# One RWKV mixer: the key projection cut in two, and the chunks' preparation written in another order around the scan

## The chip, the cores and the metric

The program runs on one core of a Trainium2 chip. The metric is the device time of one execution in microseconds (us), lower being better. The core has a matrix engine (TensorE, PE in the profile), a vector engine (VectorE, DVE), a scalar engine (ScalarE, ACT), GpSimd (POOL) and the queues that issue transfers (SP above all, and ACT). Each of them works through its own list of instructions in the order in which they stand, and waits where an input or a buffer is not there yet.

## The reference

Two layers on 256 context and 256 latent tokens of width 1024: attention with a mixture of experts, then an RWKV-7 mixer with a mixture of experts. The change lies in the mixer alone:

```python
r = heads(mix(0) @ w_r)
k = heads(mix(2) @ w_k)
v = heads(mix(3) @ w_v)
kk = k * heads(k_k)
kk = kk * lax.rsqrt(jnp.maximum(jnp.sum(kk * kk, axis=-1, keepdims=True), 1e-24))
for d in range(2):
    ...
    ins = (r, decay, k_d, v, -kk, kk * iclr)
    s_ctx, y_c = wkv_scan(zero, *(t[:, :L] for t in ins), reverse=reverse)
    _, y_l = wkv_scan(s_ctx, *(t[:, L:] for t in ins), reverse=reverse)

def step(s, inp):
    r_t, w_t, k_t, v_t, a_t, b_t = inp
    sa = jnp.einsum('bhvk,bhk->bhv', s, a_t)
    s = s * w_t[:, :, None, :] + sa[..., None] * b_t[:, :, None, :] + v_t[..., None] * k_t[:, :, None, :]
    return s, jnp.einsum('bhvk,bhk->bhv', s, r_t)
```

There are 16 heads of 64 and two directions `d`; the recurrence runs over the context tokens, then over the latent ones.

## The kernel before

The mixer is a list of steps in `rwkv` (L1236), each a function. The list is the order in which the program is written down. A scheduler then sets the order on each engine: it takes an instruction when its inputs are there by its own reckoning, the earlier-written one first, and it gives buffers of a pool out in written order. So where a step stands in the list also decides which buffer it has to wait for.

- `l` (`loras`): decay and learning-rate projections, stored to DRAM as `sgs` and `ics`. Their pool `loras` is closed at `h`; the pools `solve` and `hats` take its memory.
- `K` (`proj_k`): the key projection in four column groups n = 0 to 3. Each is a string of matmuls (L148 to L150, three for one product in full precision) and a closing part, `k_sink`: squares, head sums (L1410), a power on POOL, transposes (L1419), a spread of the factor over 64 rows (L1424), a product (L1425), and stores to `kks`. The closing part works in two PSUM banks, tag `k`.
- `R`, `gate`, `V`: the other projections. `R` evicts into tiles of the tags `kr` and `k1`, four buffers each, which `k_sink` uses too (L1404, L1440), `gate` also (L1542). All accumulators have the four PSUM banks of tag `L`; `V` needs all four at once.
- `H0` to `H3` (`wkv_hat`): for a chunk u of 128 tokens of each direction, four hat groups (direction d by half kh of the heads). A group loads `kk`, `sig`, `icl`, takes the decay sums on PE (L1585, in tag `k` while the projections run), exponentials on ACT, products on DVE and POOL, stores `hA` and `hB`, and closes with 16 matmul rows (L1624, G below) that ACT evicts into the chunk's matrix `AB[u]`. In H0 and H1 all groups share one set of buffers (`Ep`, `Em`, `A`, `BK`, `icl` one each), so they follow one another.
- `S0` to `S3` (`wkv_solve`): the inverse of a chunk's triangular matrices: 65 DVE rows in a chain (one transpose, 62 small products and sums at L1658 and L1660, two transposes), then four short runs on PE (L1682, L1686) with ACT between.
- `c0` to `c7` (`wkv_scan`): the eight scan steps of 64 tokens, each needing the state `Z` of the one before (last rows L1835 or L1838) and the solve of its chunk: S0 for c0 and c1, S1 for c2 and c3, S2 for c4 and c5, S3 for c6 and c7. `M4` to `M7` prepare the last four.
- `close`: the projections' pools end; the solves' PSUM bank and the scan's pools open.

Of the kernel before, what the change touches and what calls it, by code (L numbers as in the profile page):

```python
# [28 lines left out]
def shape_constants():  # L29
    c = {}  # L30
    t = np.arange(256)
    pos = np.stack([t // 64, t % 64], -1).astype(np.float32)
    inv = (np.float32(10000.0) ** (-np.arange(16, dtype=np.float32) / np.float32(16))).astype(np.float32)
    ang = (pos[:, :, None] * inv).astype(np.float32)
    cos, sin = np.cos(ang).astype(np.float32), np.sin(ang).astype(np.float32)
    c["cos"] = np.stack([cos, cos], 2).reshape(2, 128, 64).transpose(1, 0, 2).reshape(128, 128)
    c["sin"] = np.stack([-sin, sin], 2).reshape(2, 128, 64).transpose(1, 0, 2).reshape(128, 128)
    i, j = np.arange(128)[:, None], np.arange(128)[None, :]
    c["band"] = np.concatenate([np.where(j <= i, 0, NEG), np.where(j >= i, 0, NEG)], 1)
    c["ident"] = np.eye(128)  # L40
    c["before"] = i < j
    c["iota"] = np.broadcast_to(np.arange(384), (128, 384))
    e = np.arange(16)
    c["erev"] = np.broadcast_to(16 - e, (128, 16))
    c["grev"] = np.broadcast_to(4 - np.arange(4), (128, 4))
    lt = np.arange(128) % 64
    lc = np.arange(128) // 64
    tri = np.zeros((2, 128, 2, 65))
    for q in range(2):
        inq = (lc == q)[:, None]  # L50
        t = np.arange(64)[None, :]
        m0 = (lt <= 31)[:, None] * inq
        m1 = (lt >= 32)[:, None] * inq
        tri[0, :, q, 0:1] = -1.0 * m0
        tri[0, :, q, 1:65] = (lt[:, None] <= t) * inq - 1.0 * m0
        tri[1, :, q, 0:64] = (lt[:, None] >= t) * inq - 1.0 * m1
        tri[1, :, q, 64:65] = -1.0 * m1
    c["tri0"], c["tri1"] = tri[0].reshape(128, 130), tri[1].reshape(128, 130)
    t = np.arange(64)[None, :]
    c["gm0"], c["gm1"] = lt[:, None] <= t, lt[:, None] >= t  # L60
    c["gmk"] = np.where(np.arange(128)[:, None] < 64, lt[:, None] > t, lt[:, None] < t)
    c["e4"] = (i == np.arange(256)[None, :] // 64)
    c["hsel"] = (i // 64 == np.arange(2)[None, :])
    late = ("tri0", "tri1", "gm0", "gm1", "gmk", "hsel", "e4")
# [15 lines left out]
class Net:  # L80
# [1107 lines left out]
    def rwkv(self, st, se, sf):  # L1188
# [44 lines left out]
        lo = self.pool(slo, "loras", side="right")  # L1233
        self.Z, self.main, self.y2, self.late, wk = [None, None], {}, [], [], None
        self.trit = "k"
        for o in ["l", "K", "h", "H0", "R", "H1", "Vm", "gate", "V", "hx", "close", "S0", "H2", "S1", "c0", "H3", "x", "S2", "c1", "S3", "c2", "c3", "M4", "n", "c4", "M5", "c5", "M6", "c6", "M7", "c7", "F"]:  # L1236
            u = int(o[1]) if len(o) == 2 and o[1].isdigit() else None
            if o == "h":
                slo.close()
                vp.append(self.pool(ssv, "solve", side="right"))  # L1240
                hp["w"] = self.pool(shat, "hats", side="right")
                self.abd(hp["w"])
                self.hp = [hp["w"]]
            elif o == "hx":
                shx.close()
                hp["x"] = self.pool(shat, "hatsX", side="right")
                self.abd(hp["x"])
                self.hp = [hp["x"], hp["w"]]
            elif o == "close":
                sproj.close()  # L1250
                self.open_psum(smain, s=1)
                self.open_psum(shat, "right", t=1)
                self.trit = "t"
                vp.append(self.pool(smain, "solveX"))
                wk = self.bk = self.pool(smain, "wkv")
                self.open_psum(smain, **{t: BUFS[t] for t in "ac" if BUFS[t]})
                self.hat_tiles("A", wk)
            elif o == "l":
                self.loras(lo, h)
            elif o == "K":  # L1260
                self.proj_k(h)
            elif o == "R":
                self.proj_r(h)
            elif o == "V":
                if not V:
                    V.append(self.mix_split(3, h))
                self.proj_v(*V[0])
            elif o == "Vm":
                V.append(self.mix_split(3, h))
            elif o == "gate":  # L1270
                self.gate_hidden(h)
            elif o[0] == "H":
                q = int("0011"[u])
                self.AB.append(vp[q].tile([128, 2, 16, 64], F32, tag="AB", bufs=2 if q == 0 else 2, name=self.uid("AB")))
                self.wkv_hat(u, self.AB[-1])
            elif o[0] == "S":
                self.wkv_solve(vp[int("0101"[u])], u, self.AB[u])
            elif o == "x":
                shat.close()
                self.open_psum(smain, "right", m=2)  # L1280
                self.alias = {k: v.split() for k, v in {"y": "a"}.items()}
                self.wl = self.pool(smain, "wkvL")
                self.hat_tiles("R", self.wl)
                y2 = self.wl.tile([128, 2, D], F32, name="y2")
                self.y2 = [y2[:, t, :] for t in range(2)]
            elif o == "n":
                ssv.close()
                nring = self.pool(st, "ringN", bufs=1, side="right")
                yy = nring.tile([128, 2, D], F32, tag="yf", bufs=3, name="yy")
                y += [yy[:, t, :] for t in range(2)]  # L1290
                self.rings((nring, 1))
            elif o[0] == "M":
                self.main[u] = self.wkv_mains(wk, u)
            elif o[0] == "c":
                self.wkv_scan(wk, u, y)
            elif o == "F":
                tail = self.out_factors(nring)
# [87 lines left out]
                    ws = slice(b * width, (b + 1) * width)  # L1385
                    yield m * c + a + b, wh[:, ws], wl[:, ws]

    def proj_k(self, h):
        mh, ml = self.mix_split(2, h)
        for n in range(4):  # L1390
            acc = [self.ps(tag="L") for _ in range(2)]
            for k, wh, wl in self.wsplit("rwkv_w_k", n, 256):
                for q in range(2):
                    qs = slice(q * 128, q * 128 + 128)
                    self.mm3(acc[q], wh[:, qs], wl[:, qs], mh[k], ml[k], k == 0, k == KT - 1)
            self.k_sink(n, acc)

    def k_sink(self, n, acc):
        nc = self.nc
        pn = self.ps((128, 4, 2, 2), tag="k")  # L1400
        out = []
# [15 lines left out]
        pt = self.ps((4, 512), tag="k")  # L1417
        for t in range(4):
            nc.tensor.transpose(pt[:, t * 128:(t + 1) * 128], rn[:, t, :], self.ident)  # L1419
        rT = self.lp.tile([4, 512], F32, tag="rT", bufs=2, name=self.uid("rT"))  # L1420
        nc.vector.tensor_copy(rT, pt)
        for i, ts in enumerate(out):
            pb = self.ps(tag="k")
            nc.tensor.matmul(pb, self.cst("e4")[0:4, i * 128:i * 128 + 128], rT, start=True, stop=True)  # L1424
            nc.vector.tensor_tensor(out=ts[0], in0=ts[0], in1=pb, op=ALU.mult)  # L1425
            for a, t in enumerate(ts):
                nc.scalar.dma_start(out=self.kks[:, a, 2 * n + i], in_=t.rearrange("p (v t) -> p v t", v=2))
# [123 lines left out]
    Bs = {0: slice(0, 64), 1: slice(64, 128)}  # L1551
    Ks = {0: slice(64, 128), 1: slice(0, 64)}

    def wkv_hat(self, u, AB):
        nc = self.nc
        CD = float(np.exp(np.float32(-0.5)))
        lat = u >= 2
        for d in range(2):
# [6 lines left out]
            mid, end = (0, 64) if d == 0 else (64, 0)  # L1565
            v4 = lambda t: t.rearrange("p k (c t) -> p k c t", c=2)
            fm = self.fm[d, u]
            for kh in range(2):
                wk = self.hp[(2 * d + kh) % len(self.hp)]
                ks = slice(4 * kh, 4 * kh + 4)  # L1570
                kk = self.ht(wk, "kk", [128, 2, 4, 128])
# [45 lines left out]
                nc.vector.tensor_tensor(out=kd, in0=kd, in1=icl, op=ALU.mult)  # L1617
                nc.gpsimd.tensor_tensor(out=bk(Ks), in0=v4(kd), in1=Em[:, :, :, inc], op=ALU.mult)
                nc.sync.dma_start(out=self.hB[d, u][:, :, ks, :], in_=BK)
                for lc in range(2):  # L1620
                    p = self.ps((128, 4, 128), tag="G")
                    q64 = slice(64 * d, 64 * d + 64)
                    for q in range(4):
                        nc.tensor.matmul(p[q64, q, :], BK[:, lc, q, Bs] if d == 0 else A[:, lc, q, :],  # L1624
                                         Abd[:, lc, q].rearrange("p a t -> p (a t)"),
                                         start=True, stop=True, skip_group_check=True)
                    pq = p.rearrange("p q (a t) -> p (q a) t", a=2)
                    for jb in range(2):
# [490 lines left out]
```

## Time and profile before

| | before |
|---|---|
| median of 3 runs | 1976.08 us (1969.65 to 1979.23) |
| the profiled execution | 1968.82 us |
| its span, first to last instruction | 1967.0 us |
| PE busy over the span | 1703.4 us, 87% |
| DVE, ACT, POOL busy | 972.1, 729.0, 321.9 us |
| mean granted TensorE clock | 0.936 |

The span is what the trace shows, some 2 us less than the execution's time. The mixer runs from about 908 to 1440 us; ahead of it and behind it the two mixtures of experts stream weights.

### The profile page before, as it was taken

What the parts mean: (1) busy time and instruction counts of PE and PEld (TensorE: products, weight loads), DVE (VectorE), ACT (ScalarE), POOL (GpSimd) and SP (SyncE); (2) the same over time, 40 slices, a digit from 0 to 9 for tenths busy, and PEclk for the clock granted to TensorE, in tenths of its full rate; (3) what the DMA queues carried; (4) which work ended last, traced back from release to release, by engine and by line L of the source; (5) the groups of instructions that cost most, each with busy time, mean ns of one, the idle gap of its engine ahead of it and who ended that gap; (6) DMA issues with size and microseconds to landing.
All of it is one profiled execution on the core that took longest, in us unless ns stands there. A gap on an engine that the chain in (4) does not pass through costs nothing. (4 is left out here: it accounts for less than half of the span.)

```text
span 1967.0 us, 30330 instructions
## 1 busy us (share of the span) xinstructions
PE 1703.4 (87%) x11673; PEld 1037.8 (53%) x11673; DVE 972.1 (49%) x1864; ACT 729.0 (37%) x1379; POOL 321.9 (16%) x313
## 2 busy tenths in 40 slices
PE   5978997889999999994898978889777999988986
PEld 3845565645555555552577767879653333322321
DVE  2466555756555555657745589973653111110101
ACT  2324543545444554543545765642141000100000
POOL 2040032000000000014557353510330000000000
PEclk7989998899999999997898987889988999999999
DMA  8377766699999999995357878635395999999996
GB/s 335 108 295 255 264 186 236 224 356 410 409 410 410 407 409 365 378 361 150 108 186 226 274 209 239 197 102 125 120 392 225 409 409 409 410 408 409 409 409 274
DMA packets 232019, 585.95 MB, mean 298 GB/s; under 512 B 43131, under 2 KB 87443, under 8 KB 231862
## 3 DMA queue, kind: packets, MB, share of 16 engines
q1 hardware_dynamic: 213446, 545.46, 75.2%
q10 hardware_dynamic: 15536, 27.92, 3.9%
q0 software_dynamic: 2880, 10.49, 1.5%
q8 instruction: 96, 1.57, 0.3%
q14 instruction: 61, 0.50, 0.1%
HBM read 544.19 MB, written 39.63 MB: 297 GB/s over the span
## 5 line engine op out<-in xcount | busy, mean ns | idle before, releaser
L143 DVE TENSOR_TENSOR lo<-raw,hi 128x512 fp32r<-128x512 f32 x456 | 305.2, 713 | 208.3 <-ACT hi L142 203.1
L142 ACT ACTIVATE hi<-raw 128x512 fp32r<-128x512 f32 x488 | 292.3, 628 | 215.2 <-PE ps L150 148.1
L1122 PE MATMUL ps<-raw,XT 128*64 128x512 f32 x1024 | 233.5, 597 | 15.3 <-DMA raw<-in_moe_w_dram 15.3
L1122 PEld LDWEIGHTS ps<-raw,XT 128*64 128x64 f32 x1024 | 72.2, 136 | 170.2 <-issue 125.6
L1128 DVE TENSOR_TENSOR h<-h,ps 128x512 f32<-128x512 f32 x16 | 11.0, 688 | 303.9 <-PE ps L1122 303.9
L1140 PE MATMUL ps<-raw,hT 128*64 128x512 f32 x512 | 120.2, 607 | 15.9 <-DVE hT L1133 9.4
L1986 PE MATMUL ps<-raw,XT 128*64 128x512 f32 x512 | 122.7, 600 | 0.0
L148 PE MATMUL ps<-hi,xh 128*128 128x512 f32 x256 | 100.8, 417 | 19.6 <-ACT hi L142 15.6
L149 PE MATMUL ps<-lo,xh 128*128 128x512 f32 x256 | 106.1, 414 | 0.3
L150 PE MATMUL ps<-hi,xl 128*128 128x512 f32 x256 | 102.5, 401 | 0.0
L259 POOL TENSOR_TENSOR rs<-rs,mh 128x2 f32<-128x2 f32 (+2 forms) x5 | 3.9, 772 | 533.9 <-DVE rs L258 533.9
L1140 PEld LDWEIGHTS ps<-raw,hT 128*64 128x64 f32 x512 | 35.2, 138 | 80.4 <-issue 55.2
L1932 POOL DMA_INDIRECT G<-rowbuf,ix x12 | 13.2, 1100 | 392.7 <-DVE oh L1953 261.3
L148 PEld LDWEIGHTS ps<-hi,xh 128*128 128x128 f32 x256 | 49.5, 195 | 48.1 <-ACT hi L142 21.5
L227 PE MATMUL ps<-raw,cv 128*32 128x256 f32 x768 | 61.5, 421 | 9.1 <-DMA raw<-in_ada_w_dram 5.5
L1986 PEld LDWEIGHTS ps<-raw,XT 128*64 128x64 f32 x512 | 34.0, 136 | 64.0 <-issue 61.5
L149 PEld LDWEIGHTS ps<-lo,xh 128*128 128x128 f32 x256 | 49.9, 195 | 24.7 <-DVE lo L143 7.6
L1127 ACT ACTIVATE h<-ps 128x512 f32<-128x512 f32 x16 | 9.6, 597 | 143.0 <-PE ps L1122 143.0
L1144 ACT ACTIVATE ye<-ps 128x512 f32<-128x512 f32 x16 | 9.6, 597 | 141.7 <-PE ps L1140 141.7
L1986 PE MATMUL ps<-raw,hT 128*64 128x512 f32 x256 | 61.3, 600 | 0.8 <-DVE hT L2059 0.8
L148 PE MATMUL ps<-hi,th 128*128 128x512 f32 x128 | 50.0, 407 | 6.2 <-ACT hi L142 6.1
L150 PEld LDWEIGHTS ps<-hi,xl 128*128 128x128 f32 x256 | 49.9, 195 | 9.4
(484 smaller groups left out, 3456.0 us busy)
## 6 DMA issues: line engine op xcount, KB each, us to landing
raw<-in_moe_w_dram SPq DMA_DIRECT2D x384, 1024.0 KB
raw<-in_ada_w_dram SPq DMA_DIRECT2D x48, 1024.0 KB
kk<-kks SPq DMA_DIRECT2D x16, 512.0 KB
hB<-BK SPq DMA_DIRECT2D x16, 512.0 KB
BKm<-hB SPq DMA_DIRECT2D x16, 512.0 KB
raw<-in_attn_w_in_dram SPq DMA_DIRECT2D x6, 1024.0 KB
raw<-in_attn_w_out_dram SPq DMA_DIRECT2D x8, 512.0 KB
ybuf<-ye ACTq DMA_DIRECT2D x8, 512.0 KB
```

The lines of the kernel that those rows point to most:

```text
L142: nc.scalar.activation(hi, src, AF.Copy)
L143: (lo_eng or nc.vector).tensor_tensor(out=lo, in0=src, in1=hi.bitcast(F32), op=ALU.subtract)
L148: mm(out, lh, rh, start=start, stop=False, skip_group_check=True)
L149: mm(out, lh, rl, start=False, stop=False, skip_group_check=True)
L150: mm(out, ll, rh, start=False, stop=stop, skip_group_check=True)
L227: nc.tensor.matmul(p[32 * q:32 * q + 32, :], self.cv[:, k, :], w[:, a, q * 256:(q + 1) * 256], start=(k == 0), stop=(k == KT - 1), skip_gr ...
L1122: nc.tensor.matmul(acc[64 * n:64 * n + 64, :], XT[:, k, e % 4 * 64:e % 4 * 64 + 64], w[:, a, n * 512:(n + 1) * 512], start=(k == 0), stop= ...
L1127: nc.scalar.activation(h, hs[0], AF.Silu)
L1128: nc.vector.tensor_tensor(out=h, in0=h, in1=hs[1], op=ALU.mult)
L1140: nc.tensor.matmul(acc[64 * n:64 * n + 64, :], hT[:, k % 4, (k // 4) * 64:(k // 4) * 64 + 64], w[:, a, n * 512:(n + 1) * 512], start=(k == ...
L1932: nc.gpsimd.indirect_dma_start(out=G, out_offset=None, in_=self.rowbuf[:, :], in_offset=bass.IndirectOffsetOnAxis(ap=idx[:, 0:1], axis=0))
L1986: nc.tensor.matmul(acc[0][64 * n:64 * n + 64, :], lhs(k), w[:, a, ns], start=(k == 0), stop=(k == KT - 1), skip_group_check=True)
```

## The change

The list of steps becomes: l, K0, h, H00, H10, K1, H01, R, H11, Vm, gate, V, hx, close, S0, S1, c0, H2, c1, H3, x, S2, S3, c2, c3, M4, and so on as before. K0 makes the key groups n = 0 and 1, K1 the other two. H00 is chunk 0 with the first half of the heads (both directions), H10 chunk 1 with that half, H01 and H11 the second half. H2 now stands behind c0, not ahead of S1; H3 behind c1; c1 ahead of S2, and S3 ahead of c2. The spread of the key's norm factor is one single-pass matmul on a high and a low part, where it was a full-precision matmul; a hat group's G writes both chunks' halves of 64 into one bank, alternating between the two halves of the rows, where it took two banks one after the other.

```diff
-    c["e4"] = (i == np.arange(256)[None, :] // 64)
+    c["e4"] = (i % 32 == np.arange(256)[None, :] // 64) * (i < 64)
...
-        for o in ["l", "K", "h", "H0", "R", "H1", "Vm", "gate", "V", "hx", "close", "S0", "H2", "S1", "c0", "H3", "x", "S2", "c1", "S3", "c2", "c3", "M4", "n", "c4", "M5", "c5", "M6", "c6", "M7", "c7", "F"]:
-            u = int(o[1]) if len(o) == 2 and o[1].isdigit() else None
+        for o in ["l", "K0", "h", "H00", "H10", "K1", "H01", "R", "H11", "Vm", "gate", "V", "hx", "close", "S0", "S1", "c0", "H2", "c1", "H3", "x", "S2", "S3", "c2", "c3", "M4", "n", "c4", "M5", "c5", "M6", "c6", "M7", "c7", "F"]:
+            u = int(o[1]) if o[1:].isdigit() else None
...
-            elif o == "K":
-                self.proj_k(h)
+            elif o[0] == "K":
+                self.proj_k(h, (2 * u, 2 * u + 1))
...
-                self.wkv_hat(u, self.AB[-1])
+                self.wkv_hat(u, self.AB[u], (0, 1) if len(o) == 2 else (int(o[2]),))
...
+        self.mk = self.mix_split(2, h)
+        self.e4 = self.lp.tile([36, 256], F32R, name="e4r")
+        nc.scalar.activation(self.e4, self.cst("e4")[0:36, :], AF.Copy)
+        self.rT = [self.lp.tile([36, 512], F32R, name=f"rT{i}") for i in range(2)]
+        for t in self.rT:
+            nc.gpsimd.memset(t.bitcast(F32), 0.0)
+        self.proj_k_part(ns)
...
-        rT = self.lp.tile([4, 512], F32, tag="rT", bufs=2, name=self.uid("rT"))
-        nc.vector.tensor_copy(rT, pt)
+        rT = self.rT[n % 2]
+        nc.scalar.activation(rT[0:4, :], pt, AF.Copy)
+        nc.vector.tensor_tensor(out=rT[32:36, :], in0=pt, in1=rT[0:4, :].bitcast(F32), op=ALU.subtract)
...
-            nc.tensor.matmul(pb, self.cst("e4")[0:4, i * 128:i * 128 + 128], rT, start=True, stop=True)
+            nc.tensor.matmul(pb, self.e4[:, i * 128:i * 128 + 128], rT, start=True, stop=True)
...
-            for kh in range(2):
+            for kh in khs:
...
-                for lc in range(2):
-                    p = self.ps((128, 4, 128), tag="G")
-                    q64 = slice(64 * d, 64 * d + 64)
-                    for q in range(4):
-                        nc.tensor.matmul(p[q64, q, :], BK[:, lc, q, Bs] if d == 0 else A[:, lc, q, :],
+                p = self.ps((128, 4, 128), tag="G")
+                for q in range(4):
+                    for lc in range(2):
+                        nc.tensor.matmul(p[64 * lc:64 * lc + 64, q, :], BK[:, lc, q, Bs] if d == 0 else A[:, lc, q, :],
```

On PE, between the end of the `R` projection and the first row of `V`, the order before has one G (the two L1624 rows, further up between the gate's L1539 rows) and then the gate's transposes and `V`:

```order
L1585 MATMUL ps_9388<-C_8332,sig_9382 128x130 x2
L1585 MATMUL ps_9393<-C_8332,sig_9382 128x130 x2
L1539 MATMUL ps_10059<-g_10079,mx_10089 128x160
L1539 MATMUL ps_10060<-g_10079,mx_10089 128x160
L1539 MATMUL ps_10059<-g_10079,mx_10093 128x160
L1539 MATMUL ps_10060<-g_10079,mx_10093 128x160
L1545 MATMUL ps_10099<-C,gs_10097 128x128
L1546 MATMUL ps_10099<-C,gs_10097 32x128
L1545 MATMUL ps_10106<-C,gs_10104 128x128
L1546 MATMUL ps_10106<-C,gs_10104 32x128
L148 MATMUL ps_10111<-hi_10117,mxh_10011 128x512
```

The order of the change has there, on PE, the second, third and fourth G (L1637), the closing part of key group n = 2 (L1423, L1432, L1438) and the head sums of n = 3; the gate's transposes and the first row of `V` come right behind:

```order
L1637 MATMUL ps_9149<-Abd,A_9134 64x128 x8
L1599 MATMUL ps_9219<-C_8332,sig_9213 128x130 x2
L1599 MATMUL ps_9224<-C_8332,sig_9213 128x130 x2
L1637 MATMUL ps_9198<-Abd,BK_9186 64x128 x8
L1423 MATMUL ps_9329<-C_8332,ksq_9332 128x2 x4
L1423 MATMUL ps_9329<-C_8332,ksq_9342 128x2 x4
L1637 MATMUL ps_9246<-Abd,A_9231 64x128 x8
L1432 MATMUL ps_9353<-C,rn_9350 4x128 x4
L1438 MATMUL ps_9360<-rT_8830,e4r 128x512
L1438 MATMUL ps_9365<-rT_8830,e4r 128x512
L1423 MATMUL ps_9440<-C_8332,ksq_9443 128x2 x4
L1423 MATMUL ps_9440<-C_8332,ksq_9453 128x2 x4
```

So three hat groups and a key group's closing part moved ahead of `V` on PE, where one hat group stood.

On ACT the change puts `R`'s last evictions (L1455, tiles `ro` in the tags that `k_sink` uses) and the gate's sigmoid (L1557) behind the stores of key group n = 2 (L1441), and these behind the fourth group's evictions (L1644):

```order
L1644 ACTIVATE AB_9162<-ps_9246 32x512
L1644 ACTIVATE AB_9162<-ps_9246 32x8x32
L1434 ACTIVATE rT_8830<-ps_9353 4x512
L1441 DMA kks<-kr_9330 128x512
L1441 DMA kks<-kr_9340 128x512
L1455 ACTIVATE ro_9763<-ps_9625 128x512
L1456 DMA rsc<-ro_9763 128x512
L1455 ACTIVATE ro_9907<-ps_9769 128x512
L1456 DMA rsc<-ro_9907 128x512
L1557 ACT_TABLE_LOAD
L1557 ACTIVATE gs_10095<-ps_10057 128x160
L1434 ACTIVATE rT_8831<-ps_9464 4x512
```

Before, `R`'s evictions stand ahead of the first hat group on ACT.

On DVE, the fourth solve ends, before, ahead of scan step c3's last state rows (L1837, L1838):

```order
L1820 COPY UV_12491<-ps_12567 64x512
L1662 STREAM_TRANSPOSE TV_12072<-T_12003 128x32x32
L1663 STREAM_TRANSPOSE TU_12071<-T_12003 128x32x32
L1738 TENSOR_TENSOR LR_12653<-ps_12654,C_8332 128x512
L1837 TENSOR_TENSOR Z_12622<-ps_12605,Z_12410 128x512
L1820 COPY UV_12491<-ps_12586 64x512
L1738 TENSOR_TENSOR LR_12653<-ps_12660,C_8332 128x512
L1838 TENSOR_TENSOR Z_12622<-Z_12622,F_12494 128x512
L1837 TENSOR_TENSOR Z_12642<-ps_12625,Z_12430 128x512
L1838 TENSOR_TENSOR Z_12642<-Z_12642,F_12494 128x512
```

In the change its rows (S_11992, T_11993, W_11994) run on between the rows of the next step, c4 (UV_12728, Z_12893):

```order
L1834 COPY UV_12728<-ps_12838 64x512
L1672 TENSOR_TENSOR W_11994<-S_11992,T_11993 128x192
L1674 TENSOR_TENSOR T_11993<-T_11993,W_11994 128x8x24
L1834 COPY UV_12728<-ps_12857 64x512
L1752 TENSOR_TENSOR LR_12924<-ps_12931,C_8332 128x512
L1672 TENSOR_TENSOR W_11994<-S_11992,T_11993 128x175
L1674 TENSOR_TENSOR T_11993<-T_11993,W_11994 128x7x25
L1672 TENSOR_TENSOR W_11994<-S_11992,T_11993 128x156
L1851 TENSOR_TENSOR Z_12893<-ps_12876,Z_12612 128x512
L1674 TENSOR_TENSOR T_11993<-T_11993,W_11994 128x6x26
L1852 TENSOR_TENSOR Z_12893<-Z_12893,F_12731 128x512
L1672 TENSOR_TENSOR W_11994<-S_11992,T_11993 128x135
```

So the last part of S3 moved from ahead of c3's end to between the rows of c4, and it ends ahead of c5. Three counts from the order of the change, for the prediction: of S0's 65 DVE rows 41 stand behind `V`'s last copy (18 before); of S3's 65 rows 43 stand behind c3's last Z row, 33 of these ahead of c4's (none before); and the first sums of H01 on PE (L1599) stand behind 62 of `V`'s 192 matmuls.

## Rows read from the trace of the kernel before

**Rows 1.** Windows: us, PE, PEld, DVE, ACT, POOL busy (count), clock, DMA share, GB/s.
```profile
1074.00:1093.00 19.00, 11.84 (x69) 10.30 (x69) 14.47 (x21) 16.99 (x37) 11.58 (x12) 0.82 0.79 243
1093.00:1154.40 61.40, 61.33 (x330) 50.12 (x328) 44.15 (x77) 42.66 (x94) 21.36 (x25) 1.00 0.79 243
1158.70:1317.50 158.80, 129.04 (x2291) 115.34 (x2292) 144.68 (x289) 98.46 (x188) 64.50 (x82) 0.80 0.73 199
1317.50:1339.30 21.80, 21.80 (x591) 20.76 (x593) 8.86 (x14) 7.49 (x13) 1.80 (x4) 1.00 0.52 122
1339.30:1362.80 23.50, 22.94 (x473) 21.38 (x470) 8.82 (x14) 6.58 (x12) 2.26 (x4) 1.00 0.56 114
1362.80:1388.50 25.70, 24.56 (x488) 22.80 (x487) 11.14 (x15) 6.28 (x11) 6.66 (x5) 1.00 0.36 105
1388.50:1416.00 27.50, 26.77 (x414) 19.62 (x413) 15.03 (x24) 2.98 (x5) 5.21 (x7) 1.00 0.10 28
```
**Rows 2.** Timeline of PE, 1070 to 1159: start, us, line, operands, count, idle before.
```profile
1070.12 0.71 PE L1585 MATMUL ps<-C,sig 128*128 128x130 f32 x4 [0.55 <-DVE kr L1425]
...
1081.11 3.23 PE L1624 MATMUL ps<-Abd,BK 128*64 128x128 f32 x16 [0.34 <-DVE BK L1609]
...
1092.93 0.47 PE L148 MATMUL ps<-hi,mxh 128*128 128x512 f32 x1
...
1116.94 1.96 PE L1624 MATMUL ps<-Abd,A 128*64 128x128 f32 x16
...
1124.26 1.96 PE L1624 MATMUL ps<-Abd,BK 128*64 128x128 f32 x16
...
1153.99 0.39 PE L150 MATMUL ps<-hi,mxl 128*128 128x512 f32 x1
...
1156.81 1.96 PE L1624 MATMUL ps<-Abd,A 128*64 128x128 f32 x16 [2.43 <-ACT Abd L1612]
```
**Rows 3.** Timeline of PE and DVE, 1056 to 1071: the last key group's closing.
```profile
1056.31 1.84 PE L1410 MATMUL ps<-C,ksq 128*128 128x2 f32 x16
...
1065.12 1.98 PE L1424 MATMUL ps<-rT,C 4*128 4x512 f32 x4
...
1069.39 1.27 DVE L1425 TENSOR_TENSOR kr<-kr,ps 128x512 f32<-128x512 f32 x2
```
**Rows 4.** Timeline of ACT, POOL and SP, 1049 to 1056: the loras' end.
```profile
1049.90 0.89 ACTq L1526 DMA_DIRECT2D ics<-so  x2
...
1055.00 0.96 POOL L1321 MEMSET Abd<- 128x1024 f32 x1 [1.38 <-DMA ics<-so]
...
1055.02 0.68 SPq L1572 DMA_DIRECT2D kk<-kks  x1
...
1055.31 0.60 ACT L1441 ACTIVATE ro<-ps 128x512 f32<-128x512 f32 x1 [3.02 <-PE ps L150]
```
**Rows 5.** Timeline of DVE, 1158 to 1318: V's last copy, S0's last row, c3's last.
```profile
1158.00 0.68 DVE L1455 COPY vo<-ps 128x512 f32<-128x512 f32 x1
...
1171.62 1.94 DVE L1663 STREAM_TRANSPOSE TU<-T 128x1024 f32<-128x1024 f32 x1
...
1316.84 0.69 DVE L1838 TENSOR_TENSOR Z<-Z,F 128x512 f32<-128x512 f32 x1
```
**Rows 6.** Groups of DVE by line, 1118 to 1320: count, busy us, mean ns.
```profile
L1660 DVE TENSOR_TENSOR T<-T,W 128x31 f32<-128x31 f32 (+15 forms) x124 | 52.7, 427 | 2.5
L1658 DVE TENSOR_TENSOR W<-S,T 128x31 f32<-128x31 f32 (+15 forms) x124 | 50.2, 407 | 4.1 <-POOL T L1653 1.3
```
**Rows 7.** Timeline of PE: one run of S3, and matmuls that alternate between the halves.
```profile
1317.43 1.20 PE L1682 MATMUL ps<-TV,AB 32*32 32x32 f32 x64
...
1371.16 1.04 PE L1711 MATMUL ps<-hatA,BKm 128*64 128x128 f32 x14
```
**Rows 8.** Windows of 5 us behind the end of R; columns as in rows 1.
```profile
1075.00:1080.00 5.00, 1.94 (x10) 1.71 (x11) 4.83 (x6) 4.94 (x12) 4.25 (x5) 0.69 0.87 267
1080.00:1085.00 5.00, 4.66 (x24) 4.12 (x24) 3.37 (x4) 4.27 (x12) 3.47 (x4) 0.62 0.79 223
```

More of the change, by code (lines that the diff above doesn't have):

```diff
@@ L1273, in rwkv @@
                 q = int("0011"[u])
-                self.AB.append(vp[q].tile([128, 2, 16, 64], F32, tag="AB", bufs=2 if q == 0 else 2, name=self.uid("AB")))
-                self.wkv_hat(u, self.AB[-1])
+                if u == len(self.AB):
+                    self.AB.append(vp[q].tile([128, 2, 16, 64], F32, tag="AB", bufs=2, name=self.uid("AB")))
+                self.wkv_hat(u, self.AB[u], (0, 1) if len(o) == 2 else (int(o[2]),))
             elif o[0] == "S":
@@ L1386, in wsplit, with proj_k, proj_k_part @@
                     yield m * c + a + b, wh[:, ws], wl[:, ws]
-    def proj_k(self, h):
-        mh, ml = self.mix_split(2, h)
-        for n in range(4):
+    def proj_k(self, h, ns):
+        if ns[0]:
+            return self.proj_k_part(ns)
+        nc = self.nc
+        self.mk = self.mix_split(2, h)
[5 more added lines that the diff above has]
+        self.proj_k_part(ns)
+    def proj_k_part(self, ns):
+        mh, ml = self.mk
+        for n in ns:
             acc = [self.ps(tag="L") for _ in range(2)]
@@ L1552, with wkv_hat @@
     Ks = {0: slice(64, 128), 1: slice(0, 64)}
-    def wkv_hat(self, u, AB):
+    def wkv_hat(self, u, AB, khs):
         nc = self.nc
@@ L1619, in wkv_hat @@
                 nc.sync.dma_start(out=self.hB[d, u][:, :, ks, :], in_=BK)
-                for lc in range(2):
-                    p = self.ps((128, 4, 128), tag="G")
-                    q64 = slice(64 * d, 64 * d + 64)
-                    for q in range(4):
-                        nc.tensor.matmul(p[q64, q, :], BK[:, lc, q, Bs] if d == 0 else A[:, lc, q, :],
+                p = self.ps((128, 4, 128), tag="G")
+                for q in range(4):
+                    for lc in range(2):
+                        nc.tensor.matmul(p[64 * lc:64 * lc + 64, q, :], BK[:, lc, q, Bs] if d == 0 else A[:, lc, q, :],
                                          Abd[:, lc, q].rearrange("p a t -> p (a t)"),
                                          start=True, stop=True, skip_group_check=True)
-                    pq = p.rearrange("p q (a t) -> p (q a) t", a=2)
+                pq = p.rearrange("p q (a t) -> p (q a) t", a=2)
+                for lc in range(2):
                     for jb in range(2):
@@ L1630, in wkv_hat @@
                         nc.scalar.activation(AB[rows, lc, 8 * kh:8 * kh + 8, 0:64 - 32 * jb],
-                                             pq[rows, :, 32 * jb:64], AF.Copy)
+                                             pq[64 * lc + 32 * jb:64 * lc + 32 * jb + 32, :, 32 * jb:64], AF.Copy)
                 if lat:
```

## The prediction

> **What bounds the kernel now.** I read the windows of the page first, to find the stretches of the mixer with different limits, then the timelines of PE, ACT and DVE in each. Four stretches matter. (1) Up to about 1074 PE works through the loras, K and R. (2) From 1074 to 1093 it has only the first hat group and the gate: 11.8 of 19 us busy. (3) From 1093 to 1154.4 V runs, with PE busy all the time and six hat groups' G among its rows. (4) From V's last copy, 1158.7, to the last state of c3, 1317.5, DVE is the bound: 144.7 of 158.8 us busy with S0's end, S1, S2, S3, H2, H3 and four scan steps. Then c4 to c7 take 21.8 to 27.5 us each, PE busy nearly throughout at the full clock, DVE for 9 to 15 us [rows 1, 5]. What lies behind 1416 isn't touched.
>
> **The start of the hats.** H00 needs only K0, but it can't begin much sooner than H0 did: its buffers lie in the loras' memory. The loras' last stores are issued at 1049.9 and have landed when POOL clears the hats' tile at 1055.0; the first load follows at 1055.0 [rows 4]. By these rows a transfer takes some 4.7 us from issue to landing, so H00's first sums can run at about 1061 (estimate; bounds 1057 and 1070). H0's ran at 1070.1, held by the last key group in the tag k [rows 2]. Gain: 9 us. The first G came 11.0 us after the first sums (1070.1 to 1081.1), which gives 1072.
>
> **What then stands ahead of V.** This is where I see the loss. In written order K1's closing parts come behind H00 and H10, and both work in the two banks of tag k. So K1's head sums must wait until the fourth hat group's sums are read, and the order shows them between the third G and the fourth. And R's and the gate's results go into tiles that K1's closing part still holds, so ACT evicts R behind the stores of n = 2, and V needs the PSUM banks that R then frees. Before, PE began V after one G.
>
> Three more groups: the first three intervals took 35.8 us (1081.1 to 1116.9), the four later ones 39.9 us (to 1156.8), 10.0 each [rows 2]. The alternating G is shorter: L1711 has G's shape and alternates the halves, and takes 1.04 / 14 = 0.074 us a row where G takes 1.96 / 16 = 0.123 [rows 2, 7], so 0.8 us a group, 2 us over three. I take 30 - 2 = 28 us: the fourth G at 1100 (bounds: three of the shortest interval, 1116.9 to 1124.3, 22 us; 36 us). Then the closing part: 14.4 us from the head sums to the end of the product (1056.3 to 1070.7) [rows 3], of which 1.5 us run ahead of the fourth G: 1113. The store lands 4.7 us later, 1118; two evictions of 0.6 us [rows 4], a table load and the sigmoid, which I put at 1.5 us together by the same row: 1120. **V starts at 1120 in place of 1093, 27 us later** (bounds 1105 and 1135).
>
> The stretch of V gets shorter, not by its matmuls but by four hat groups in place of six: two groups of some 3 us each (G and sums) and 0.8 us from each of the four are 9 us, so PE alone would take 52 us. But H01 starts behind 62 of V's 192 matmuls, 17 us, and its four groups take 11 + 30 - 2 = 39 us more: 56 us, with the last G's 1.2 us some 58. V's end: 1178 in place of 1154.4. **+24 us** (bounds: 1105 + 52 gives +3, 1135 + 62 gives +43).
>
> The spread of the norm factor costs 1.98 us per key group now [rows 3]; in a single pass the nearest row of that width is V's, 0.39 us [rows 2], so 1.2 us less PE each. It is hidden: K0's two lie ahead of the loras' end, K1's two in a wait for ACT. Two memsets, a copy of e4 and one more small row per group lie beside other work too; if uncovered, the small row adds 0.7 us per group to the closing part. I count all this as nothing, bounds -3 and +1.
>
> **The clock.** With PE mostly waiting in 1075 to 1080 the granted clock was 0.69, then 0.62, between the two levels of 1.2 and 2.4 GHz, and back at full speed in V [rows 1, 8]. In the change the wait is more than twice as long, so V may open at the lower level: 10 us at 0.65 cost 3.5 us. I put it in the range and not in the sum, since H01's groups and not PE set V's end. The Trainium skill, "TensorE: Matmul & The Clock Gate" (Part 1), says that the throttled clock is the default and that activity releases it; the trace agrees (0.62 after the waits, 1.00 in V). By that rule V would open throttled and the sum be 3.5 us more.
>
> **The stretch that DVE bounds.** Its work is the same but for two ends. S0 starts only when H01 is done, now late in V, so 41 of its rows stand behind V's last copy where 18 did: 23 rows of 0.417 us (mean of L1658 and L1660 [rows 6]), +9.6 us. 43 rows of S3 go out of it, 41 small ones and two transposes of 1.94 us [rows 5]: -21.0. Two rows of M4, 0.69 each by the last row of [rows 5], come in: +1.4. **-10 us**, as long as DVE idles as little as now, 14 us (bound: 6 us more, for c0 now stands behind nearly all of S1). So c0 ends later than now, not earlier: the change doesn't bring the scan forward.
>
> **The tail.** In c4 33 rows of S3 add 13.8 us to 8.9 us of DVE: 22.7 against a step of 21.8 [rows 1]. In-order waits make it some 24, +2 us. S3's four PE runs of 1.2 us [rows 7] now lie in c5, where PE was busy for 22.9 of 23.5 us: +5 us. They left c4, but there DVE is the bound now. **+7 us** (bounds 0 and +9).
>
> **Sum.** 24 - 10 + 7 = +21 us. The profiled execution took 1968.8 us (span 1967.0), so 1990; it lay 7.3 us below the median of the runs, 1976.1. On the median: 1997 us. Adding the bounds: 3 - 10 + 0 - 3 = -10, 1966; and 43 - 4 + 9 + 1 = +49, 2025, the 3.5 us of the clock within V's 62.
>
> **The rivals.** One per cent of this time is 20 us; about 0.5%, 10 us, is what a measurement can tell from no change: below 1966 faster, above 1986 slower.
>
> - *V late, scan late* (the sum): 1997. For it: the order, which can't be got round, and intervals of eight measured groups. Against it: those ran beside V's splits on ACT and DVE, and the first ones now won't. Chance 0.64.
> - *A quick chain, no change*: with fewer splits beside them the groups follow each other in 7.3 us, the fourth G is at 1094, V starts at 1112 and ends at 1167, +13; S3 hides wholly in c4 and c5: 13 - 10 + 3 = +6, 1982. For it: 7.3 us did occur. Against it: ACT alone was busy for 17 of 19 us at the first group. Chance 0.24.
> - *Faster, by S3*: if V ends no later than 1159, the 21 us of S3 that leave the DVE stretch win: 4 - 10 + 0 - 3 = -9, 1967 or less. It decides at a V start of about 1105. For it: DVE is the bound of 159 us, and those rows surely leave it. Against it: the closing part and its store alone hold V until 1105 even with the shortest intervals. Chance 0.12.
>
> Slower 0.64, same 0.24, faster 0.12. Range 1972 to 2018: it leaves out the fastest half of the third case and the upper bounds.
>
> **What would show it.** In the trace of the change: the first L1599 near 1061; L1637 of the fourth group near 1100, with L1423 just ahead; a PE mostly idle from 1074 to V's first row near 1120; V's last near 1178; S0's last transpose some 39 us behind V's last copy, where it was 15; c3's last Z row near 1331; c4 and c5 longer, c6 and c7 as now. Wrong would be: V starting by 1105, hat groups under 8 us apart, or scan steps c0 to c3 that wait for something else than DVE.

## The result, and the profile after

The changed kernel takes 2004.0 us (median of 4 runs, 2003.3 to 2010.95), the kernel before 1977.65 beside it: a ratio of 1.0148, 95% interval 1.0110 to 1.0186. That is 26.4 us slower between the medians (the ratio compares the means, 29 us apart); 21 us, 1997, was forecast. The profiled execution took 2003.43 us (span 2001.7). One execution of the kernel before (2273 us) and one of the last kernel below (2262 us) had a granted clock of 0.72, where all others had 0.92 to 0.94, and count for no ratio.

First the windows of the changed kernel, stage by stage; columns as in [rows 1]. The stages are: the first hat group; the wait for V; V to its last copy on DVE; the DVE stretch to c3's last state; then c4 to c7.

```profile
1058.00:1077.00 19.00, 14.05 (x82) 12.90 (x83) 17.39 (x17) 14.30 (x31) 15.06 (x14) 0.69 0.70 216
1077.00:1113.50 36.50, 20.32 (x123) 17.25 (x121) 11.65 (x19) 21.62 (x42) 12.87 (x12) 0.59 0.65 211
1113.50:1173.60 60.10, 55.54 (x296) 44.04 (x294) 34.49 (x58) 33.99 (x71) 18.16 (x21) 0.97 0.61 190
1173.60:1344.60 171.00, 126.50 (x2233) 114.71 (x2234) 133.05 (x270) 93.73 (x182) 65.32 (x82) 0.73 0.67 181
1344.60:1366.60 22.00, 20.61 (x418) 19.23 (x412) 20.24 (x47) 4.76 (x8) 0.43 (x3) 1.00 0.52 118
1366.60:1397.70 31.10, 28.12 (x695) 26.20 (x694) 13.93 (x24) 14.17 (x21) 3.20 (x5) 0.89 0.39 87
1397.70:1422.00 24.30, 24.30 (x493) 22.22 (x492) 10.13 (x14) 7.13 (x12) 4.35 (x4) 1.00 0.38 111
1422.00:1451.00 29.00, 27.99 (x418) 20.67 (x416) 15.34 (x24) 2.97 (x5) 7.00 (x7) 1.00 0.10 26
```

Against [rows 1]: PE is busy for only 20.3 of the 36.5 us ahead of V; the stretch behind V took 158.8 us and takes 171.0, although DVE has 11.6 us less to do in it (133.05 for 144.68); in c4 DVE is now busy for 20.2 of 22.0 us, and c5 takes 31.1 us where it took 23.5. The three sums are +15 at V's last copy (1158.7 to 1173.6), +12 in the stretch, +8 in c4 to c7 (98.5 to 106.4): the 35 us between the two spans. This is more than the 26 between the medians, because the profiled execution of before lies 9 us below the median of 1977.65 and this one 0.6 below its own. 5 of the 15 us stand ahead of the mixer: its first matmul starts at 943.13 here and at 937.91 before, and in the twelve other traces below at any time from 938.5 to 946.0. Counted from there, V's last copy comes 230.5 us into the mixer where it came 220.8 in: +10.

The wait for V, in the timeline of PE in the changed kernel:

```profile
1058.33 1.02 PE L1599 MATMUL ps<-C,sig 128*128 128x130 f32 x4 [2.89 <-DMA icl<-ics]
...
1066.69 1.09 PE L1637 MATMUL ps<-Abd,BK 128*64 128x128 f32 x16 [0.95 <-DVE BK L1623]
...
1081.01 1.09 PE L1637 MATMUL ps<-Abd,A 128*64 128x128 f32 x16
...
1091.67 1.97 PE L1637 MATMUL ps<-Abd,BK 128*64 128x128 f32 x16 [6.18 <-DVE BK L1623]
1093.58 3.57 PE L1423 MATMUL ps<-C,ksq 128*128 128x2 f32 x16
1098.52 1.97 PE L1637 MATMUL ps<-Abd,A 128*64 128x128 f32 x16 [1.37 <-ACT Abd L1626]
1103.05 1.01 PE L1432 MATMUL ps<-C,rn 128*4 128x128 f32 x4 [2.56 <-POOL rn L1428]
1105.46 1.22 PE L1438 MATMUL ps<-rT,e4r 36*128 36x512 f32 x2 [1.39 <-DVE rT L1435]
...
1113.46 0.78 PE L148 MATMUL ps<-hi,mxh 128*128 128x512 f32 x1
```

And on ACT, from the store of key group n = 2 to the gate:

```profile
1107.00 0.92 ACTq L1441 DMA_DIRECT2D kks<-kr  x2
1109.06 0.60 ACT L1455 ACTIVATE ro<-ps 128x512 f32<-128x512 f32 x1 [4.37 <-DMA kks<-kr]
...
1111.04 1.28 ACT L1557 ACT_TABLE_LOAD   x1 [0.39 <-ACT ro L1455]
1112.34 0.30 ACT L1557 ACTIVATE gs<-ps 128x160 f32<-128x160 f32 x1
```

Four G stand ahead of V, the closing part's head sums (L1423) between the third and the fourth; R's eviction waits for the store to leave the tile, as the bracket behind 1109.06 says, and V for the gate behind it. This is the chain that the prediction read from the order.

### The profile page after: what moved, and what is told of

It reads as the page before. It is cut to its first block, busy times and chain, and to the rows that moved or that the text cites. A ratio compares the mean times of both kernels' runs of the same rounds, so it can differ in the third digit from the quotient of the medians.

```text
span 2001.7 us, 30292 instructions
## 1 busy us (share of the span) xinstructions
PE 1702.3 (85%) x11665; PEld 1040.5 (52%) x11665; DVE 969.1 (48%) x1864; ACT 735.3 (37%) x1386; POOL 320.3 (16%) x315
## 5 line engine op out<-in xcount | busy, mean ns | idle before, releaser
L150 PE MATMUL ps<-hi,xl 128*128 128x512 f32 x256 | 102.9, 403 | 0.0
```

The source lines that it names most:

```text
L150: mm(out, ll, rh, start=False, stop=stop, skip_group_check=True)
```

## The experiments

All times are medians beside runs of the kernel before on the same chip (1975.1 to 1976.4 there). Each ratio is against the kernel before beside it. First four kernels that take the change apart: its late order (all behind `close`), its early order (K0 to H11), its local edits (single-pass spread, alternating G), and the place of K1 in the early order.

**The early order with the local edits, without the late order.**

```diff
-... "close", "S0", "S1", "c0", "H2", "c1", "H3", "x", "S2", "S3", "c2", "c3", "M4" ...
+... "close", "S0", "H2", "S1", "c0", "H3", "x", "S2", "c1", "S3", "c2", "c3", "M4" ...
```

> The changed kernel with the steps behind close in the order of before (S0 H2 S1 c0 H3 x S2 c1 S3 c2 c3 M4); K0, H00, H10, K1, H01, R, H11 stay. Theory (both parts cost): V and S0 end as in the changed kernel, 1170 and 1208; the DVE stretch is 158.8 + 23 rows of 0.42 = 168 to 170 us with idle time of 14 us again; the tail of 8 us is gone: 2004 - 2 - 8 = 1994 us (1990 to 1998). Rival A (the late order alone costs, the later V is made up for behind it): 1976 to 1981. Rival B (the early part is the whole loss, the late order gains 10 us as predicted): 2008 or more.

Measured: 2002.9 us, ratio 1.0138 (1.0123 to 1.0154). The loss is all there without the late order. The time lies in none of the three ranges: rival A falls; B's "the early part is the whole loss" holds, but the late order neither gains nor loses behind it (2004.0 with it). The stretch is longer than the theory had it, 183.4 us, since DVE idles for 31 us of it (183.36 - 152.60) and not for 14:

```profile
1171.84:1355.20 183.36, 145.28 (x2452) 129.49 (x2452) 152.60 (x314) 101.72 (x192) 65.34 (x83) 0.68 0.64 169
1355.20:1448.29 93.09, 91.22 (x1794) 79.75 (x1789) 43.26 (x62) 20.96 (x36) 14.54 (x18) 1.00 0.38 94
```

**Late order alone, in the kernel before.**

```diff
-... "close", "S0", "H2", "S1", "c0", "H3", "x", "S2", "c1", "S3", "c2", "c3", "M4" ...
+... "close", "S0", "S1", "c0", "H2", "c1", "H3", "x", "S2", "S3", "c2", "c3", "M4" ...
```

> The kernel before with only the steps behind close in the order of the change (S0 S1 c0 H2 c1 H3 x S2 S3 c2 c3 M4). V and S0 end as before (1154, 1174). Theory: the idle time of DVE, 24 us more, belongs to this order (S2 and S3 wait for a G that ACT evicts behind S1's and S2's results, and the last Z of c0 and c2 stand behind a solve's matmuls on PE): stretch 158.8 - 20 + 24 = 163, tail +8: 1976 + 12 = 1988 us (1983 to 1992). Rival (the idle time comes from the late V and S0): stretch 139 to 145, tail +8: 1962 to 1970.

Measured: 1966.4 us, ratio 0.9957 (0.9940 to 0.9974): the rival's range, and the theory falls. The idle time of DVE doesn't belong to the late order by itself (14.0 us here: 135.78 - 121.78). The windows show the term as the prediction priced it, S3's rows out of the stretch (158.8 to 135.8 us), and c4 to c7 giving half of it back (98.5 to 110.9):

```profile
1169.15:1304.93 135.78, 112.38 (x2025) 101.58 (x2024) 121.78 (x246) 87.49 (x174) 65.38 (x81) 0.87 0.85 228
1304.93:1415.83 110.90, 104.23 (x2218) 90.89 (x2216) 61.66 (x109) 34.20 (x55) 16.38 (x19) 0.97 0.33 85
```

**The local edits alone.**

```diff
-... "l", "K0", "h", "H00", "H10", "K1", "H01", "R", "H11", ... "S0", "S1", "c0", "H2", "c1", "H3", "x", "S2", "S3", ...
+... "l", "K0", "K1", "h", "H0", "R", "H1", ... "S0", "H2", "S1", "c0", "H3", "x", "S2", "c1", "S3", ...
```

> The changed kernel with all steps in the order of before (K0 K1 h H0 R H1 ... S0 H2 S1 c0 H3 x S2 c1 S3 c2 c3 M4): what is left of the change is the single-pass spread, the alternating G and the rT tiles. Theory: nothing that can be measured, 1974 to 1979 us, G at 0.08 us a row in place of 0.123. Rival: the extra row on DVE and the ACT copy in the closing part delay the hats: 1981 or more.

Measured: 1957.4 us, ratio 0.9911 (0.9896 to 0.9926), the fastest kernel of the study, and outside of both expectations. The edits shorten what they touch by little; but the scheduler reckons with these lengths, and although the steps are written as before, 41 of S3's DVE rows now stand behind c3's last Z. On DVE in this kernel, 1298 to 1300, one can see S3's rows (L1672, L1674) between c3's Z rows (L1851, L1852), where before S3 was done 5 us ahead of the last of them (1312.1 and 1317.5). The second fence has its windows:

```profile
1298.49 0.69 DVE L1851 TENSOR_TENSOR Z<-ps,Z 128x512 f32<-128x512 f32 x1
1299.10 0.40 DVE L1672 TENSOR_TENSOR W<-S,T 128x240 f32<-128x240 f32 x1
1299.41 0.69 DVE L1852 TENSOR_TENSOR Z<-Z,F 128x512 f32<-128x512 f32 x1
1300.02 0.40 DVE L1674 TENSOR_TENSOR T<-T,W 128x240 f32<-128x240 f32 x1
```

```profile
1159.06:1300.10 141.04, 115.29 (x2106) 102.97 (x2106) 129.37 (x258) 93.97 (x185) 65.81 (x83) 0.82 0.79 216
1300.10:1405.55 105.45, 101.16 (x2152) 88.61 (x2150) 58.74 (x104) 31.26 (x51) 16.14 (x19) 1.00 0.35 94
```

**K1's closing part ahead of the half hats**, with the steps behind `close` in the order of before (the diff is against the first experiment).

```diff
-... "K0", "h", "H00", "H10", "K1", "H01", "R", "H11", ...
+... "K0", "K1", "h", "H00", "H10", "H01", "R", "H11", ...
```

> The order of before behind close, and ahead of it K0 K1 h H00 H10 H01 R H11: the closing part of K1 stands ahead of the half hats, not behind four of them. Theory (what holds V is the closing part behind the fourth group, by tag k and R's tiles): two groups stand ahead of V, V starts at 1095 to 1100 and ends at 1158 to 1163: 1978 to 1983 us. Rival (the order of the half hats itself holds V): V starts at 1110 or later, 1990 us or more.

Measured: 1985.0 us, ratio 1.0051 (1.0035 to 1.0067), 2 us above the theory's range. Against the first experiment only K1's place differs: 18 us less. V starts at 1088.8, 148.5 us into the mixer in place of 171.9, and its last copy comes at 210.9 in place of 232.9. So the closing part behind four hat groups is what held V. But the rest of the time stays lost: the stretch takes 177.3 us, 29 of them idle on DVE. From the local edits alone this kernel differs only in the hats, which come there whole (H0 R H1) and here by halves in turn (H00 H10 H01 R H11). Its V ends 5.5 us sooner into the mixer, and still it takes 27.5 us more: DVE idles 29 us of the stretch for 12, and S3's 41 rows are back in it (busy 148.1 us for 129.4). So the early order loses in two ways: by K1's place, which holds V, and by the halves in turn, which lengthen the stretch.

Four more kernels ask what the stretch pays for, and what the half hats do to it.

**Both gains together**: the local edits and the late order, K0 K1 h H0 R H1 ahead.

> The changed kernel with K0 K1 h H0 R H1 in the order of before ahead of close, and the late order of the change behind it: the two parts that gained alone (19 and 10 us) together. Theory (both gain by the same thing: c0 and c1 run ahead of the end of S1's chain, and most of S3's DVE rows, 48 here, stand behind c3's last Z): the same gain once, 1955 to 1962 us. Rival (the local edits gain for a reason of their own): the sum, 1945 to 1950 us.

Measured: 1966.6 us (1955.6 to 1968.4), ratio 0.9953 (0.9937 to 0.9970). They don't add up: no run reaches the rival's range. But the median misses the theory's range too, by 5 us. Whether the late order costs something on top of the edits stays open, since these runs spread by 13 us where those of the local edits alone spread by 4.

**H2 behind c0, and c1 ahead of S2**, each in the kernel before.

```diff
-... "S0", "H2", "S1", "c0", "H3", "x", "S2", "c1", "S3", "c2", "c3", ...
+... "S0", "S1", "c0", "H2", "H3", "x", "S2", "c1", "S3", "c2", "c3", ...
```

> The kernel before with S1 and c0 ahead of H2 (S0 S1 c0 H2 H3 x S2 c1 S3 c2 c3). In the DVE order c0's last Z now stands ahead of 26 of S1's rows (before: none), but all of S3's rows stay ahead of c3's last Z. Theory A (the rows of S3 that leave the stretch are the gain): no gain, 1972 to 1979 us. Theory B (a scan step that needn't wait for the end of the next solve on PE and DVE is the gain): 1960 to 1968 us.

```diff
-... "S0", "H2", "S1", "c0", "H3", "x", "S2", "c1", "S3", "c2", "c3", ...
+... "S0", "H2", "S1", "c0", "c1", "H3", "x", "S2", "S3", "c2", "c3", ...
```

> The kernel before with c1 ahead of H3, S2 and S3 (S0 H2 S1 c0 c1 H3 x S2 S3 c2 c3). In the DVE order 22 of S3's rows now stand behind c3's last Z, and c0's last Z still behind all of S1. Theory A (S3's rows): 22 x 0.42 = 9 us less in the stretch, 3 to 6 us more in the tail: 1970 to 1974 us. Theory B (c0 ahead of S1's end): no gain, 1975 us or more.

Measured: 1986.4 us, ratio 1.0056 (1.0036 to 1.0076), and 1974.9 us, ratio 1.0001 (0.9988 to 1.0015). With H2 behind c0, c0 ends at 1217.1, 35 us behind S0 where it took 57; the time isn't shorter but 10 us longer. So theory B falls: with all of S3 still ahead of c3 on DVE, an early c0 gains nothing here. Theory A had no change in place of a loss, and what loses the 10 us isn't shown. With c1 ahead, DVE has 12 us less to do, but idles 8 more, and c4 to c7 give 4 back: theory A's mechanism without its gain. Rows of S3 that leave the stretch aren't a gain by themselves.

**Chunk 0's halves first**, K1 behind two hat groups.

```diff
-... "K0", "h", "H00", "H10", "K1", "H01", "R", "H11", ...
+... "K0", "h", "H00", "K1", "H01", "R", "H10", "H11", ...
```

> The changed kernel with H01 ahead of R and H10 and H11 behind it (K0 h H00 K1 H01 R H10 H11): chunk 0 is done first, and K1's closing part stands behind two hat groups in place of four. Theory (the four groups and the closing part ahead of V, and the late H01, move S0's end, which sets the time): V starts some 18 us sooner, at 152 us behind the mixer's first matmul in place of 170, S0 ends as much sooner, c0 stands ahead of S1's end: 1976 to 1986 us. Rival (the late start of S0 is bound by V, behind which 40 of its rows stand either way): 1994 us or more.

Measured: 1994.1 us, ratio 1.0092 (1.0074 to 1.0110). V starts 13 us sooner (157.2 us into the mixer, for 170.3), not 18, and S0 ends 19 us sooner; but all of S3's rows are back in the stretch (178.8 us, DVE busy for 157.1), and the products of two hat groups more (L1608 runs ten times in it, eight in the change), which the expectation had not counted. By its number the rival came true; that the cause it names is what sets the time isn't shown.

The last four: the two local edits one by one, and the place of S0 with K1 ahead in both.

**The alternating G alone; the single-pass spread alone**, both in the order of before.

> The kernel before with the alternating G alone. The shorter rows shift the scheduler's reckoning, so 19 of S3's rows now stand behind c3's last Z (before none, all local edits together 41). Theory A (the gain is the S3 rows that leave the stretch): half of the gain of all the local edits or less, 1966 to 1973 us. Rival (the faster G is the gain): 1960 us or less.

> The changed kernel with the order of before everywhere and the G of before: the spread in a single pass alone. 3 of S3's rows stand behind c3's last Z. Theory A: no change, 1972 to 1978 us. Rival (the shorter closing part of a key group is the gain): 1962 us or less.

Measured: 1967.3 us, ratio 0.9961 (0.9945 to 0.9976), and 1972.5 us, ratio 0.9977 (0.9962 to 0.9991). Each gives a part, the one with 19 rows out more than the one with 3; neither rival's number is reached, and both times lie in theory A's ranges. But that the rows of S3 are the gain is not shown: 22 rows out gained nothing above, 45 gained 10 us, 41 gained 19.

**S0 early or late, K1 ahead of the hats, late order of the change.**

```diff
-... "K0", "h", "H00", "H10", "K1", "H01", "R", "H11", ...
+... "K0", "K1", "h", "H00", "H01", "R", "H10", "H11", ...
```

> The changed kernel with K0 K1 h H00 H01 R H10 H11 ahead of close, its late order kept: the hat groups are split by halves as in the change, but chunk 0's four come first, and K1's closing part ahead of them. 19 of S0's rows stand behind V's last copy (before 18, change 41), 32 of S3's behind c3's last Z. Theory (S0's end sets the time): S0 ends within 20 us of V's last copy, DVE idles 10 to 16 us from there to c3: 1960 to 1970 us. Rival (the split of the hats by itself costs): 1980 us or more.

```diff
-... "K0", "h", "H00", "H10", "K1", "H01", "R", "H11", ...
+... "K0", "K1", "h", "H00", "H10", "H01", "R", "H11", ...
```

> As the run above, with the halves of the two chunks in turn as in the change: K0 K1 h H00 H10 H01 R H11. 46 of S0's rows stand behind V's last copy, 29 of S3's behind c3's last Z. Theory: V starts and ends as in the run above, S0 ends 15 us or more later, DVE idles 25 us or more from there to c3: 1980 to 1990 us. Rival (V's end and the rows of S3 set the time, S0's place doesn't): within 5 us of the run above.

Measured: 1976.2 us, ratio 1.0001 (0.9984 to 1.0017), and 1974.1 us, ratio 0.9985 (0.9968 to 1.0002). My theory that S0's end sets the time falls: S0 ends 25 us later into the mixer in the second (251.7 for 226.9), and the times are within 2 us, as the rival of the second run has it. DVE does S1's rows while it can't do S0's (20 of them stand ahead of S0's end, 1 in the first); the stretch is 10 us longer (164.4 for 154.6, idle 30 for 20), and c4 to c7 are 11 us shorter (101.7 for 112.3).

The second of these is also the plainest experiment on the change: it is the changed kernel with one name of the list moved, K1 to the front of H00, and takes **30 us less** (1974.1 for 2004.0; each against the kernel before beside it, 28). V's first row and the stages behind it there:

```profile
1092.79 0.47 PE L148 MATMUL ps<-hi,mxh 128*128 128x512 f32 x1
```

```profile
1156.48:1320.85 164.37, 126.24 (x2240) 114.12 (x2240) 134.20 (x290) 93.87 (x182) 64.48 (x82) 0.75 0.71 193
1320.85:1422.52 101.67, 97.03 (x2002) 85.17 (x2001) 55.29 (x91) 28.70 (x46) 15.45 (x18) 0.98 0.35 83
```

V starts 149.0 us into the mixer in place of 170.3, and its last copy stands 212.7 us in, 18 sooner. The other 11 us lie in the stretch (7) and in c4 to c7 (5). Against "both gains together" it differs only in the hats, by halves in turn and not whole: 8 us more, idle 30 us for 9.

All of them side by side, from the windows and the DVE order of each kernel (us; V's last copy counted from the mixer's first matmul; idle is the stretch less DVE's busy time). All columns but the median and the rows come from one profiled execution each, which lies within 1 us of the median for most kernels, but 11 us below it for "edits and late order", 7 for the spread alone and for before, 5 for "K1 ahead, S0 early, late order", and 3 above for the late order. Differences of a few us between them tell nothing:

| kernel | median | V's last copy | stretch | DVE busy | idle | c4 to c7 | S0 rows behind V | S3 rows behind c3 |
|---|---|---|---|---|---|---|---|---|
| before | 1976 | 220.8 | 158.8 | 144.7 | 14 | 98.5 | 18 | 0 |
| local edits | 1957 | 216.4 | 141.0 | 129.4 | 12 | 105.5 | 24 | 41 |
| late order | 1966 | 223.2 | 135.8 | 121.8 | 14 | 110.9 | 18 | 45 |
| edits and late order | 1967 | 209.2 | 134.6 | 125.4 | 9 | 117.7 | 24 | 48 |
| G alone | 1967 | 217.5 | 153.3 | 142.4 | 11 | 101.0 | 24 | 19 |
| spread alone | 1972 | 210.8 | 155.2 | 144.8 | 10 | 105.0 | 23 | 3 |
| c1 ahead of S2 | 1975 | 222.2 | 155.2 | 133.0 | 22 | 102.9 | 18 | 22 |
| H2 behind c0 | 1986 | 223.8 | 165.8 | 145.5 | 20 | 98.5 | 18 | 0 |
| K1 ahead, S0 early, late order | 1976 | 212.1 | 154.6 | 134.7 | 20 | 112.3 | 19 | 32 |
| K1 ahead, late order | 1974 | 212.7 | 164.4 | 134.2 | 30 | 101.7 | 46 | 29 |
| K1 ahead | 1985 | 210.9 | 177.3 | 148.1 | 29 | 101.5 | 46 | 0 |
| chunk 0 first, late order | 1994 | 219.6 | 178.8 | 157.1 | 22 | 97.7 | 40 | 0 |
| early order | 2003 | 232.9 | 183.4 | 152.6 | 31 | 93.1 | 41 | 0 |
| the change | 2004 | 230.5 | 171.0 | 133.1 | 38 | 106.4 | 41 | 43 |

## Why the prediction came out as it did

The direction, the size within 7 us and the cause of V's delay were right: the early order, and in it K1's closing part behind four hat groups, holds V. Moving K1 alone gives back 18 us (early order) or 28 to 30 us (the change). But that the sum came so near is luck: two of its terms were wrong in opposite directions, V's end (+24 forecast, +15 measured) and the stretch behind it (-10 forecast, +12 measured).

**The start of the hats**: 1061 forecast, 1058.3 measured; the first G at 1066.7, not 1072.

**What stands ahead of V**: the fourth G at 1098.5 (forecast 1100), 31.8 us behind the first (forecast 28). The closing part takes 14.0 us, from 1093.58 to the end of its last product on DVE at 1107.57 (forecast 14.4):

```profile
1106.29 1.28 DVE L1439 TENSOR_TENSOR kr<-kr,ps 128x512 f32<-128x512 f32 x2 [0.89 <-PE ps L1438]
```

Two terms were mis-sized. The head sums run 4.9 us ahead of the fourth G, where 1.5 were put, so the product ends 9 us behind it and not 13. And R's eviction begins 1.5 us behind the product (2.1 behind the store's issue at 1107.0), where a landing of 4.7 us was put, taken from the loras' last stores [rows 4]. The evictions, the sigmoid and the gate's transposes then take 4.4 us, where 2.7 were put. So V begins at 1113.5, not 1120, and with 5 us of the mixer's own later start taken off, 15 us later into the mixer (170.3 for 155.0) and not 27.

**V's length**: its last row starts 55.5 us behind its first (forecast 56 to 58, before 61); H01's first sums come 17 us behind V's start, as forecast. V's end is +15, or +10 from the mixer's start, where +24 was forecast.

**The clock**: behind a wait at 0.59, with PE busy for 20.3 of 36.5 us, V opened with a granted clock of 0.69 in its first 5 us, between the levels of 1.2 and 2.4 GHz, and 1.00 in the next 5. That costs some 1.6 us (an estimate, 5 x 0.31), where 3.5 were put into the range. The Trainium skill, "TensorE: Matmul & The Clock Gate" (Part 1), would have V open throttled behind the wait; the trace agrees (0.69, then 1.00).

**The stretch that DVE bounds**: this is the step that failed. The work was priced well, -10 forecast and -11.6 measured. What failed is its condition, "as long as DVE idles as little as now, 14 us (bound: 6 us more ...)": it idles 38 us, 24 more. So the stretch is 12 us longer, not 10 shorter. The prediction's own list of what would be wrong has this sign, "scan steps c0 to c3 that wait for something else than DVE". Eight of the waits make 27 of the 38 us; in the changed kernel, from the timeline of DVE:

```profile
1189.60 0.69 DVE L1608 TENSOR_TENSOR A<-kk,Ep 128x512 f32<-128x512 f32 x1 [2.88 <-DMA hatA<-hA]
...
1249.76 0.69 DVE L1849 TENSOR_TENSOR Z<-ps,F 128x512 f32<-128x512 f32 x1 [4.37 <-PE ps L1844]
...
1253.45 1.93 DVE L1665 STREAM_TRANSPOSE S<-AB 128x1024 f32<-128x1024 f32 x1 [1.29 <-ACT AB L1644]
...
1299.03 0.69 DVE L1608 TENSOR_TENSOR A<-kk,Ep 128x512 f32<-128x512 f32 x1 [3.11 <-ACT Ep L1602]
...
1309.58 0.69 DVE L1851 TENSOR_TENSOR Z<-ps,Z 128x512 f32<-128x512 f32 x1 [4.64 <-PE ps L1844]
...
1313.89 0.69 DVE L1608 TENSOR_TENSOR A<-kk,Ep 128x512 f32<-128x512 f32 x1 [2.89 <-ACT Ep L1602]
...
1323.27 2.01 DVE L1665 STREAM_TRANSPOSE S<-AB 128x1024 f32<-128x1024 f32 x1 [2.77 <-ACT AB L1644]
...
1337.87 0.69 DVE L1752 TENSOR_TENSOR LR<-ps,C 128x512 f32<-128x512 f32 x1 [5.17 <-issue]
```

and what stands on PE ahead of c0's Z row at 1249.76 and, in the last line, ahead of M4's at 1337.87:

```profile
1243.55 2.43 PE L1844 MATMUL ps<-UV,tok 128*64 128x64 f32 x40
1247.19 1.92 PE L1696 MATMUL ps<-TV,AB 32*32 32x32 f32 x64 [1.21 <-ACT Q L1704]
1249.03 0.69 PE L1844 MATMUL ps<-UV,tok 128*64 128x64 f32 x6
...
1335.74 3.75 PE L1751 MATMUL ps<-hatR,BKm 128*128 128x128 f32 x16 [5.80 <-DMA hatR<-hA]
```

c0's last products (L1844) queue behind a run of S1 (L1696) that waits for ACT; S2's first row at 1253.45 waits for an eviction of H2 (L1644), S3's at 1323.27 for one of H3; c2's Z row at 1309.58 waits for the products of its own step on PE (L1844); three first products of hat groups (L1608) wait for ACT's exponentials (L1602) or a transfer; the last rows of M4 (L1752) stand ahead of c3's last Z and wait for PE, which waited 5.8 us for a load of `hatR`. Each engine keeps its order, and DVE stands at these rows until they are released.

That the order of the hats sets the idle time is shown: with whole hats it is 12 us (local edits) and 9 (edits and late order), and with nothing else changed in the list but the halves in turn, 29 and 30. It isn't V's lateness, since in the last two V ends earlier than before (210.9 and 212.7 us into the mixer, for 220.8). By which path the halves do it stays open. Late S0 rows go with it: four of the five kernels in which 40 or more of S0's rows stand behind V idle for 29 to 38 us, the fifth 22, the nine others 9 to 22. But this is a pattern and not a cause shown, and idle time isn't always lost: the pair with S0 early and late differs by 10 us of it and gets them back in c4 to c7. The granted clock of the stretch is 0.68 to 0.76 in the five and 0.79 to 0.87 in the nine; whether PE's lower clock makes the waits longer or follows from them stays open.

**The tail**: +7 forecast, +7.9 measured; c4 hardly longer (22.0 for 21.8), c5 7.6 us longer.

**The local edits**: "I count all this as nothing, bounds -3 and +1". Alone they gain 19 us. I looked for the cost of the edited rows and not for what their lengths do to the order that the scheduler writes: 41 rows of S3 move about as far as the late order moves them. Whether these rows are the gain isn't shown. Together with the late order the edits gain no more than it does alone (1966.6 for 1966.4). It does mean that the change hides a kernel some 45 us faster than itself (1957.4 for 2004.0).

**The rivals**: the quick chain's first intervals didn't occur (14.3, 10.7 and 6.8 us between the four G; and by the prediction's own 20 us from the fourth G to V it should have had V at 1114, not 1112). "Faster, by S3" had its mechanism right, as the late order alone shows with 10 us; but it needed a V start by 1105, which K1's place forbade, and an idle time that didn't grow.

## What to carry to other kernels

Where a closing part shares buffers or PSUM banks with work that stands ahead of it in written order, look for what its last store releases: here one name in a list, moved ahead of four hat groups, was worth 28 to 30 us. An edit that only changes lengths can reorder a scheduled program far behind it, so compare the orders of the whole program before costing it at nothing. And of a stretch that an engine bounds, price the idle time as carefully as the work: here 12 us of work left it, and it got 12 us longer.

## Not expected

G with its rows alternating between the two halves took 1.09 us for 16 rows, 0.068 us a row (0.123 before [rows 2]), less even than the 0.074 that the forecast took from L1711; in the wait for V, at a granted clock of 0.59, it took 1.97. The same program part, K0 K1 h H0 R H1 to V's last copy, with PE's rows in the same order, took 216.4 us in one execution and 209.2 in another (local edits without and with the late order), so that single profiles of this kernel can't be compared below some 7 us.
